# Per-token input normalisation behind two interleaved GLA blocks, a pooling map one block later, and a token-major last FFN slice, in a two-layer hybrid decoder kernel

## The chip, the cores and the metric

The kernel runs on all 8 cores of one Trainium2 chip. Each core takes one prompt of 2048 tokens and 16 samples of 8 tokens (one more tile of 128 tokens), and the cores do not exchange data. The metric is the device time of the slowest core in microseconds (us). A run is called fast when the two dies agree, and slow when the cores of one die show a lower granted TensorE clock and take longer; only fast runs are compared here. Engine names: PE is TensorE (matmul), PEld its weight loads, DVE is VectorE, ACT is ScalarE, POOL is GpSimd, SP is SyncE, which issues most transfers here.

## The reference, cut to what matters

```python
# D_MODEL = 1024, DEPTH = 2, 2048 prompt tokens per core, 16 x 8 sample tokens
def mixer_block(h, ...):
    hn = rms_norm(h, norm_mix)
    q, k, v, g_out, g_lr, xp, u, vv, gates = split(hn @ w_in)
    g_log = log_sigmoid(g_lr @ w_gk2 + b_gk) / 16
    o, s_new = gla_mix(q, k, v, g_log, s_gla)             # A: chunked scan with a state
    branch_a = (rms_norm(o) * silu(g_out)) @ w_br_a
    pool_out = pool_mix(xp, ...)                          # B: trailing windows 2/4/8/16, then a 128x128 map per group
    branch_c = (gelu(u) * (tril(w_s) @ gelu(vv) + b)) @ w_br_c   # C: chunks of 128
    merged = sum of sigmoid(gates) * branch               # with branch_b = pool_out @ w_br_b
    return h + merged @ w_out

# then  h = h + relu(rms_norm(h) @ w_ff1)**2 @ w_ff2, per layer; a final rms_norm at the end
```

## The kernel before

The 17 tiles of 128 tokens form five blocks (3, 3, 3, 4, 4 tiles; 384 or 512 tokens). Activations are kept feature-major: features on the 128 partitions, tokens along the free axis. The residual stream `hT` is fp32, and everything that the large matmuls read is bf16. Weights (1 MB each in fp32) pass through a ring of seven slots. A layer runs in stages: GLA projections for every block with the scan in the background, then mix (pooling and spatial gating), then gates and output projection, then the FFN. `tick()` moves the background work on by one step; PE itself executes strictly in the order of issue.

The start: every x tile is loaded, transposed, normed and written to DRAM before the first projection.

```python
def load_x():
    for t in range(4): xdma(t)                    # 4 x buffers of 512 KB
    rest_consts()
    for b in range(NB):
        for j in range(nt):
            for half in range(2):
                ps = psum()
                pe_transposes([...4 blocks of 128x128 of xt...], ident, ...)
                # PSUM -> hT[b], half 0 by ACT, half 1 by DVE
            xdma(t0 + j + 4)
        na = Norm(b, V_NMIX)                      # squares on ACT, summed by ones-matmuls on PE
        for m in range(KT): na.square(m)
        spill_h(b)                                # whole block to DRAM
    for b in range(NB): norm_drain(b)

def spill_h(b):
    spq.dma(h_d[b].rearrange("p (k t) -> p k t", k=KT), hT[b][:, :, :], reads=hTk[b], writes=[h_dB[b]])
```

The mix stage: the small spatial weights are loaded late, and a block's pooled tile is awaited before its map.

```python
def mix_loads(l):                                 # called at the end of the sample GLA
    spq.dma(wsp, w_spT[l] ...)                    # 128x128 per group, fp32
    spq.dma(w8, w_spT[l][:, 0:8, 0:8] ...)        # 8x8 corners for the samples
    ...
def mix_prep(l):
    tt(wsT, wsp, mask, ALU.mult, ...)             # DVE waits for wsp
    pe_group([(ps[:, 0:32], r8, w8, True, True)], ...)   # PE waits for w8
    ...
def mix_block(l, b):
    ... xp projections -> xf; pe_ = spawn(pool())  # window sums on DVE in the background
    ... u projections, vv projections with sgate(j - 1) after vgrp(j)
    drain(pe_)
    for g in range(4):
        pe_group([(ps[:, 0:T], wpm[:, g, :], pooled[:, g, 0:T], True, True)], ...)   # PE waits for pooled
        act(OBC[:, g, 0:T], ps, AF.Copy, ...)
    sgate(nt - 1)
    spq.dma(OB_d[b], OBC ...)
```

The end: the last FFN slice produces feature-major output, which is normed with ones-matmuls, scaled, transposed and stored.

```python
def ff2(l, sl, n, b):
    for m in range(KT):
        ps = proj_fm(...)                         # 8 matmuls 128 x T
        tt(hT[b][:, m, :], hT[b][:, m, :], ps, ALU.add, ...)
        if last: na.square(m)
def store_y(b):                                   # after the final norm
    for j in range(nt):
        for half in range(2):
            pe_transposes([...4 of hT[b], fp32...], ident, ...)
            act(yt[...], ps, AF.Copy, ...)
        spq.dma(rows(y_p, y_s, t0 + j), yt)
```

Of the kernel before, what the change touches and what calls it, by code (L numbers as in the profile page):

```python
# [27 lines left out]
V_NMIX, V_NFFN, V_NFIN, V_GLAN = 0, 16, 32, 40  # L28
# [70 lines left out]
def build_program():  # L99
# [28 lines left out]
    vecs = din("vecs", [128, 48])  # L128
# [53 lines left out]
    def act(out, in_, func, reads, writes, bias=None, scale=None):  # L182
        kw = {}
        if bias is not None:
            kw["bias"] = bias
        if scale is not None:
            kw["scale"] = scale
        return op(ACT, lambda: nc.scalar.activation(out=out, in_=in_, func=func, **kw), reads, writes)  # L188
# [104 lines left out]
    vec_t = sbc("vec_t", [128, 48])  # L293
# [17 lines left out]
    phist = sbc("phist", [128, 4, 15])  # L311
    fix = sbc("fix", [128, 16])
# [34 lines left out]
    xt = [sba(f"xt{i}", [128, D], F32, RA + i * 4 * KB) for i in range(4)]  # L347
# [4 lines left out]
    lvj = [part(lv, lv.t, 2 * KB * j, 2 * KB) for j in range(4)]  # L352
# [9 lines left out]
    go = sba("go", [128, KT, 512], BF16, R1 + 52 * KB)  # L362
    H4 = sba("H4", [128, KT, 512], BF16, R1 + 60 * KB)
# [20 lines left out]
    OBC = sba("OBC", [128, KT, 512], BF16, R1 + 36 * KB)  # L384
# [18 lines left out]
    ytok = [sba(f"ytok{i}", [128, D], F32, RM + 4 * KB * i) for i in range(2)]  # L403

# [9 lines left out]
    spq.dma(vec_t.t[:, :], vecs[:, :], writes=[vec_t])  # L414
# [9 lines left out]
    def rest_consts():  # L424
        spq.dma(cm.t[:, :, :], cmask[:, :, :], writes=[cm])
        spq.dma(psc.t[:, :], psc_d[:, :], writes=[psc])
        spq.dma(r8.t[:, :], r8_d[:, :], writes=[r8])
        spq.dma(mcol.t[:, :], mcol_d[:, :], writes=[mcol])
        spq.dma(invc.t[:, :, :], invc_d[:, :, :], writes=[invc])
        vcopy(ident_bf.t[:, :], ident.t[:, :], [ident], [ident_bf])  # L430
# [6 lines left out]
    def mix_consts(l):  # L437
        plq.dma(wpm.t[:, :, :], w_pm[l].rearrange("g c d -> c g d"), writes=[wpm])
        plq.dma(bsp.t[0:1, :, :], b_sp[l:l + 1], writes=[bsp])
        plq.dma(bsS.t[0:1, :, :, :], b_sp[l][:, 0:8].rearrange("(o g) t -> o g t", o=1).unsqueeze(2).broadcast_to([1, 4, NSEQ_S, LS]),  # L440
                writes=[bsS])

    def mix_loads(l):
        spq.dma(wsp.t[:, :, :], w_spT[l].rearrange("g s t -> s g t"), writes=[wsp])
        spq.dma(w8.t[:, :, :], w_spT[l][:, 0:8, 0:8].rearrange("g s t -> s g t"), writes=[w8])
# [4 lines left out]
    def mix_prep(l):  # L450
        tt(wsT.t[:, :, :], wsp.t[:, :, :], cm.t[:, 0, :].unsqueeze(1).broadcast_to([128, 4, 128]), ALU.mult, [wsp, cm], [wsT])
        ps = psum()
# [39 lines left out]
    def pump():  # L492
        while loaded[0] < len(order) and (loaded[0] < NSLOT or loaded[0] - NSLOT in retired):
# [47 lines left out]
    class Norm:  # L541
        def __init__(self, b, wcol, final=None):
            self.b, self.wcol, self.final = b, wcol, final
# [10 lines left out]
        def run(self):  # L554
# [15 lines left out]
            for kt in range(KT):  # L570
                if self.final is None:
                    dst, dB = hn_v(b)[:, kt, :], hnk[b][kt]
                else:
                    dst, dB = hT[b][:, kt, :], hTk[b][kt]
                stt(dst, hT[b][:, kt, :], vec_t.t[:, self.wcol + kt:self.wcol + kt + 1], rstd.t[:, 0:T], ALU.mult, ALU.mult,
                    [hTk[b][kt], vec_t, rstd], [dB])
                yield 1
            if self.final is not None:
                yield from self.final(b)
# [16 lines left out]

    def load_x():
        def xdma(t):
            spq.dma(xt[t % 4].t[:, :], rows(x_p, x_s, t), writes=[xt[t % 4]])
        for t in range(4):  # L600
            xdma(t)
        rest_consts()
        for b in range(NB):
            t0, nt = BLK[b]
            for j in range(nt):
                xb = xt[(t0 + j) % 4]
                for half in range(2):
                    ps = psum()
                    pe_transposes([(ps.t[:, k4 * 128:(k4 + 1) * 128], xb.t[:, (half * 4 + k4) * 128:(half * 4 + k4 + 1) * 128]) for k4 in range(4)],
                                  ident.t[:, :], [xb, ident], [ps])  # L610
                    o = hT[b][:, half * 4:half * 4 + 4, j * 128:(j + 1) * 128]
                    i = ps.t[:, :].rearrange("p (k t) -> p k t", k=4)
                    w = hTk[b][half * 4:half * 4 + 4]
                    if half == 0:
                        act(o, i, AF.Copy, [ps], w)
                    else:
                        vcopy(o, i, [ps], w)
                    tick()
                if t0 + j + 4 < NTILE:
                    xdma(t0 + j + 4)  # L620
            na = Norm(b, V_NMIX)
            norms[b] = na
            for m in range(KT):
                na.square(m)
                tick()
            spill_h(b)
        for b in range(NB):
            norm_drain(b)
# [5 lines left out]
    def gla_project(l, b):  # L634
# [5 lines left out]
        norm_drain(b)  # L640
        ps = psum()
        pe_group([(ps.t[:, 0:T], wglr.t[:, kt, :], hn_v(b)[:, kt, :], kt == 0, kt == KT - 1) for kt in range(KT)], [wglr], [ps], late=hnk[b])
        act(glr.t[0:32, 0:T], ps.t[0:32, 0:T], AF.Copy, [ps], [glr])
        tick()

        def vgrp(hf, j):
# [7 lines left out]
            act(o, ps.t[:, :], AF.Copy, [ps], [w])  # L654
            tick()

        def gate(j):
            ps = psum()
            pe_group([(ps.t[:, :], glr.t[:, j * 128:(j + 1) * 128], wgk2.t[:, :], True, True)], [glr, wgk2], [ps])
            act(lv.t[:, j, :], ps.t[:, :], AF.Exp, [ps], [lvj[j]], scale=-1.0)  # L660
            act(lv.t[:, j, :], lv.t[:, j, :], AF.Ln, [lvj[j]], [lvj[j]], bias=1.0)

        vgrp(0, 0)
        vgrp(0, 1)
        for j in range(nt):
            gate(j)
            if j >= 2:
                vgrp(0, j)
        if b == NB - 1:
            retire(l, "v0")  # L670
        for j in range(nt):
            vgrp(1, j)
        if b == NB - 1:
            retire(l, "v1")

        def cums(h):
            ps = psum()
            for j in range(nt):
                mi = 3 if (b == 0 and j == 0) else 1
                pe_group([(ps.t[:, j * 128:(j + 1) * 128], lv.t[:, j, h * 128:(h + 1) * 128], cm.t[:, mi, :], True, True)], [lvj[j], cm], [ps])  # L680
# [25 lines left out]

        cums(0)
        cums(1)
        for h in range(4):
            kgrp(h)  # L710
            qgrp(h)
            if h + 2 < 4:
                cums(h + 2)
        if b == NB - 1:
            retire(l, "k", "q")

    def gla_gate(l, b):
        T = TB[b]
        po = 128 if b == 0 else 0
        for m in range(KT):  # L720
            s, view = wget(l, "g%d" % (m // 4))
            ps = hn_fm(b, s, view, (m % 4) * 128)
            act(go.t[:, m, 0:T - po], ps.t[:, po:T], AF.Silu, [ps], [go])
# [28 lines left out]
    def gla_scan(l, b):  # L752
# [22 lines left out]
        for j in range(npr):  # L775
# [26 lines left out]
            yield from o_norm(l, OV, OB_, go.t[:, :, sl], go, H4.t[:, :, sl], H4)  # L802
# [3 lines left out]
        spq.dma(H4_d[b][:, :, po:TB[b]], H4.t[:, :, 0:TB[b] - po], reads=[H4], writes=[H4_dB[b]])  # L806
# [69 lines left out]
    def mix_block(l, b):  # L876
# [4 lines left out]
        if b == 0:  # L881
            memset(phist.t[:, :, :], 0.0, [phist])
        vcopy(xf.t[:, :, 0, 0:15], phist.t[:, :, :], [phist], [xf])
# [6 lines left out]
        vcopy(phist.t[:, :, :], xf.t[:, :, 0, Tp:Tp + 15], [xf], [phist])  # L890

# [20 lines left out]
        def pool():  # L912
            if b == 0:
                yield from pool_part(xfS, NSEQ_S, LS, 0, False)
            yield from pool_part(xf, 1, Tp, po, b == 0)

        if b == 0 or b == NB - 1:
# [9 lines left out]
        if b > 0:  # L927
            pe_ = spawn(pool())
# [5 lines left out]
        if b == 0:  # L934
# [5 lines left out]
            pe_ = spawn(pool())  # L940
# [14 lines left out]
        def sgate(j):  # L955
            smp = b == 0 and j == 0
            ps = psum()
            mms = []
            for g in range(4):
                osl = ps.t[:, g * 128:(g + 1) * 128]  # L960
                wv = wsS.t[:, g, :] if smp else wsT.t[:, g, :]
                bv = bsS.t[:, g, :, :].rearrange("o i t -> o (i t)") if smp else bsp.t[:, g, :]
                mms += [(osl, vtk.t[:, j, g * 128:(g + 1) * 128], wv, True, False, True), (osl, ones_bf.t[:, :], bv, False, True, True)]
            pe_group(mms, [vtkj[j], ones_bf] + ([wsS, bsS] if smp else [wsT, bsp]), [ps])
            tt(OBC.t[:, 4:8, j * 128:(j + 1) * 128], ps.t[:, :].rearrange("p (g t) -> p g t", g=4), uT.t[:, :, j * 128:(j + 1) * 128],
               ALU.mult, [ps, uT], [OBC])

        for j in range(nt):
            vgrp(j)
            if j > 0:  # L970
                sgate(j - 1)
        if b == NB - 1:
            retire(l, "vv")
        drain(pe_)
# [4 lines left out]
        sgate(nt - 1)  # L979
# [85 lines left out]
    def ff2(l, sl, n, b):  # L1065
# [3 lines left out]
        last = sl == 3  # L1069
        if last:  # L1070
            if b > 1:
                norm_drain(b - 2)
            na = Norm(b, V_NMIX + (l + 1) * 8) if l + 1 < DEPTH else Norm(b, V_NFIN, final=store_y)
# [10 lines left out]
        if last and l + 1 < DEPTH:  # L1084
            spill_h(b)

    def store_y(b):
        t0, nt = BLK[b]
        for j in range(nt):
            yt = ytok[(t0 + j) % 2]  # L1090
            for half in range(2):
                ps = psum()
                pe_transposes([(ps.t[:, k4 * 128:(k4 + 1) * 128], hT[b][:, half * 4 + k4, j * 128:(j + 1) * 128]) for k4 in range(4)],
# [122 lines left out]
```

## Time and profile before

Three runs gave a median of 2673.1 us: two fast ones, 2658.04 and 2673.1, and a slow one, 3045.57. In the profiled run the slowest core's span was 2655.1 us.

These are lines of the profile's page of the kernel before: busy times, the span in 40 slices (each digit is a busy share in tenths; PEclk is the granted clock in tenths), and the chain of waits by engine.

```profile
PE 2487.5 (94%) x14502; PEld 1371.0 (52%) x14502; DVE 1235.2 (47%) x2227; ACT 929.4 (35%) x1702; POOL 75.3 (3%) x94
...
PE   5798986999999999999999898699999999999997
...
PEclk7899997999999999999999999799999999999999
...
PE 86%; DMA 4%; DVE 4%; ACT 3%; issue 2%; another core or an unknown queue 0%; DVEq 0%; SPq 0%; ACTq 0%
```

PE is the bound. Its idle time and low clock lie in the first slices (start), around slices 7 and 26 (each layer's passage from GLA to mix; a slice is 66 us), and in the last slice. The view of PE's waits names the reasons (what waits, for what: us in total, times, longest):

```profile
PE ps L215 <- DVE pooled L191: 32.0, 2, 16.0
PE ps L215 <- ACT lv L188: 18.6, 24, 0.8
PE ps L215 <- DMA w<-w_spT: 16.3, 2, 9.6
...
PE ps L224 <- DMA xt_55<-xs: 8.0, 1, 8.0
PE ps L224 <- DMA xt_57<-xp: 7.0, 1, 7.0
```

The table by stretches shows the start of the slowest core (stretch, its length, then busy us and number of instructions of PE, PEld, DVE, ACT and POOL, the granted clock, the DMA share and GB/s):

```profile
0.00:100.00 100.00, 56.69 (x255) 34.19 (x255) 41.86 (x83) 43.83 (x85) 10.30 (x17) 0.80 1.02 232
100.00:133.00 33.00, 27.80 (x170) 17.27 (x171) 7.46 (x27) 8.44 (x23) 0.00 (x0) 0.90 0.73 103
```

And this is layer 1's mix stage in the same view, on core 0, from the last silu gate of the GLA projections to the first sigmoid of the gates:

```profile
1626.00:1788.00 162.00, 130.06 (x821) 73.44 (x831) 82.83 (x161) 81.38 (x141) 4.12 (x5) 0.88 0.42 91
```

So 32 of these 162 us are PE idle. Last, two groups of instructions by their form in the kernel before: first the fp32 transposes of the end, then, from the stretch 90 to 130 us, fp32 matmuls that compute a cumulative sum with a mask (count of records, busy us, mean ns of one record, which contains pipeline latency):

```profile
L224 PE MATMUL ps<-ident_t,hT_48 128*128 128x128 f32 x32 | 5.5, 348 | 3.1 <-DVE hT_48 L194 3.1
L224 PE MATMUL ps<-ident_t,hT_47 128*128 128x128 f32 x32 | 3.9, 275 | 0.9 <-DVE hT_47 L194 0.8
L224 PE MATMUL ps<-ident_t,hT_44 128*128 128x128 f32 x24 | 3.6, 273 | 0.0
...
L215 PE MATMUL ps<-cm,lv 128*128 128x128 f32 x24 | 3.8, 310 | 0.0
```

A 128x128 fp32 transpose leaves one record of roughly 0.11 us busy (3.9 us for 32).

### The profile page before, as it was taken

What the parts mean: (1) busy time and instruction counts of PE and PEld (TensorE: products, weight loads), DVE (VectorE), ACT (ScalarE), POOL (GpSimd) and SP (SyncE); (2) the same over time, 40 slices, a digit from 0 to 9 for tenths busy, and PEclk for the clock granted to TensorE, in tenths of its full rate; (3) what the DMA queues carried; (4) which work ended last, traced back from release to release, by engine and by line L of the source; (5) the groups of instructions that cost most, each with busy time, mean ns of one, the idle gap of its engine ahead of it and who ended that gap; (6) DMA issues with size and microseconds to landing.
All of it is one profiled execution on the core that took longest, in us unless ns stands there. A gap on an engine that the chain in (4) does not pass through costs nothing.

```text
span 2655.1 us, 42225 instructions; the slowest of 8 cores (2625.8 to 2655.1 us)
## 1 busy us (share of the span) xinstructions
PE 2487.5 (94%) x14502; PEld 1371.0 (52%) x14502; DVE 1235.2 (47%) x2227; ACT 929.4 (35%) x1702; POOL 75.3 (3%) x94
## 2 busy tenths in 40 slices
PE   5798986999999999999999898699999999999997
PEld 3455543554545555555555555355454555545554
DVE  3345445443435544444554545544343564444444
ACT  4366554422223321112346655542222331111144
POOL 1000000000000000000000000000000000000000
PEclk7899997999999999999999999799999999999999
DMA  9923561523518222314262347153350822221112
GB/s 243 158 88 92 117 118 48 124 88 83 117 36 195 48 33 32 48 17 65 83 131 80 100 107 128 48 109 103 74 126 32 198 49 32 33 39 27 17 49 88
DMA packets 172519, 225.72 MB, mean 85 GB/s; under 512 B 12242, under 2 KB 159866, under 8 KB 166904
## 3 DMA queue, kind: packets, MB, share of 16 engines
q0 software_dynamic: 80896, 77.97, 20.8%
q1 hardware_dynamic: 91416, 145.06, 16.9%
q8 instruction: 122, 2.00, 0.3%
q14 instruction: 85, 0.70, 0.1%
HBM read 237.46 MB, written 63.96 MB: 114 GB/s over the span
## 4 chain that ended last, share of the span: by engine, by line
PE 86%; DMA 4%; DVE 4%; ACT 3%; issue 2%; another core or an unknown queue 0%; DVEq 0%; SPq 0%; ACTq 0%
PE ps L215 85%; DMA w<-w_spT 1%; PE ps L224 1%; DMA xt_56<-xp 1%; ACT L188 1%; DMA OB_d<-OBC 1%; DMA xt_58<-xp 1%; DVE pt_101 L191 1%; DVE tmp_86 L194 0%; ACT lv L188 0%; DVE pt_102 L191 0%; ACT rsg L188 0%; DMA yp<-ytok_134 0%; DVE H_72 L191 0%
## 5 line engine op out<-in xcount | busy, mean ns | idle before, releaser
L215 PE MATMUL ps<-hn,wring 128*128 128x384 bf16 (+1 forms) x6400 | 1255.4, 350 | 12.6 <-DMA wring<-w_in 7.0
L215 PEld LDWEIGHTS ps<-hn,wring 128*128 128x128 bf16 x6400 | 625.4, 99 | 558.2 <-issue 30.0
L188 ACT ACTIVATE rl_124<-ps 128x384 f32<-128x384 f32 (+1 forms) x160 | 85.4, 534 | 498.1 <-PE ps L215 447.4
L215 PE MATMUL ps<-a_1_123,wring 128*128 128x384 bf16 (+1 forms) x1280 | 243.5, 347 | 0.0
L215 PE MATMUL ps<-a_0_122,wring 128*128 128x384 bf16 (+1 forms) x1280 | 241.2, 347 | 0.0
L215 PE MATMUL ps<-wring,hn 128*128 128x512 bf16 x848 | 206.3, 391 | 3.8 <-ACT lv L188 2.4
L215 PEld LDWEIGHTS ps<-a_1_123,wring 128*128 128x128 bf16 x1280 | 125.2, 98 | 109.9
L215 PEld LDWEIGHTS ps<-a_0_122,wring 128*128 128x128 bf16 x1280 | 125.2, 98 | 109.5
L188 ACT ACTIVATE sg_118<-ps 128x384 f32<-128x384 f32 (+1 forms) x120 | 64.1, 534 | 236.3 <-PE ps L215 156.2
L188 ACT ACTIVATE sg_119<-ps 128x384 f32<-128x384 f32 (+1 forms) x120 | 64.0, 533 | 221.2 <-PE ps L215 154.2
L188 ACT ACTIVATE rl_125<-ps 128x384 f32<-128x384 f32 (+1 forms) x160 | 85.4, 534 | 143.8 <-PE ps L215 78.5
L215 PEld LDWEIGHTS ps<-wring,hn 128*128 128x128 bf16 x848 | 82.0, 100 | 96.1 <-issue 17.1
L191 DVE TENSOR_TENSOR hT_48<-hT_48,ps 128x512 f32<-128x512 f32 x80 | 55.0, 688 | 71.4 <-PE ps L215 71.4
L191 DVE TENSOR_TENSOR hT_47<-hT_47,ps 128x512 f32<-128x512 f32 x80 | 55.0, 688 | 70.2 <-PE ps L215 70.2
L191 DVE TENSOR_TENSOR tmp_120<-sg_118,ps 128x384 f32<-128x384 f32 (+1 forms) x80 | 48.6, 607 | 81.5 <-ACT sg_118 L188 41.3
L191 DVE TENSOR_TENSOR a_0_122<-rl_124 128x384 bf16<-128x384 f32 (+1 forms) x80 | 48.9, 611 | 78.1 <-ACT rl_124 L188 78.1
L191 DVE TENSOR_TENSOR a_1_123<-rl_124 128x384 bf16<-128x384 f32 (+1 forms) x80 | 48.9, 612 | 77.0 <-ACT rl_124 L188 76.9
L191 DVE TENSOR_TENSOR tmp_121<-sg_119,ps 128x384 f32<-128x384 f32 (+1 forms) x80 | 48.5, 607 | 69.6 <-PE ps L215 35.0
L191 DVE TENSOR_TENSOR a_0_122<-rl_125 128x384 bf16<-128x384 f32 (+1 forms) x80 | 48.9, 612 | 67.6 <-ACT rl_125 L188 65.3
L191 DVE TENSOR_TENSOR a_1_123<-rl_125 128x384 bf16<-128x384 f32 (+1 forms) x80 | 48.9, 612 | 63.4 <-ACT rl_125 L188 63.4
L194 DVE SCALAR_TENSOR_TENSOR tmp_86<-ps,vec_t,rsg 128x512 f32<-128x512 f32 x68 | 51.0, 749 | 55.4 <-ACT rsg L188 51.5
L215 PE MATMUL ps<-OBs_112,wring 128*128 128x384 bf16 (+1 forms) x320 | 72.5, 349 | 3.1 <-DVE acc_114 L191 3.1
(325 smaller groups left out, 2794.9 us busy)
## 6 DMA issues: line engine op xcount, KB each, us to landing
wring<-w_ff POOLq DMA_DIRECT2D x32, 1024.0 KB, 9.1
wring<-w_in POOLq DMA_DIRECT2D x30, 1024.0 KB, 13.1
OB_d<-OBC SPq DMA_DIRECT2D x6, 768.0 KB, 4.3
H4s_110<-H_d SPq DMA_DIRECT2D x6, 768.0 KB, 8.5
OBs_112<-OB_d SPq DMA_DIRECT2D x6, 768.0 KB, 8.8
H4s_111<-H_d SPq DMA_DIRECT2D x6, 768.0 KB, 11.1
OBs_113<-OB_d SPq DMA_DIRECT2D x6, 768.0 KB, 5.0
h_d<-hT_47 SPq DMA_DIRECT2D x2, 2048.0 KB, 15.7
```

The source lines that it names most:

```text
L188: return op(ACT, lambda: nc.scalar.activation(out=out, in_=in_, func=func, **kw), reads, writes)
L191: return op(DVE, lambda: nc.vector.tensor_tensor(out=out, in0=in0, in1=in1, op=alu), reads, writes)
L194: return op(DVE, lambda: nc.vector.scalar_tensor_tensor(out=out, in0=in0, scalar=scalar, in1=in1, op0=op0, op1=op1), reads, writes)
L215: inst = nc.tensor.matmul(m[0], m[1], m[2], start=m[3], stop=m[4], **kw)
L224: inst = nc.tensor.transpose(o, i, ident_ap)
```

## The change

The change attacks all three places where PE idles, and the GLA stage on the way.

1. Start. Per-token statistics replace the ones-matmuls: ACT squares a whole token row and accumulates it, and a 128x128 matmul with a diagonal spreads the scale over partitions. The tiles are processed in the background while GLA blocks 0 and 1 are projected, interleaved. The transposed x goes to a small buffer `hx` and from there to DRAM tile by tile.
2. GLA. The silu gate has two buffers, half of the v evictions move to DVE, and a scan is not drained in a burst before the next gate.
3. Mix. The 8x8 weights are loaded at the start of the layer; the map of the pooled tile of block b is issued during block b+1.
4. End. The last FFN slice is computed token-major, with the residual added by fp32 matmuls against an identity into the same PSUM group; the final norm is then one row statistic and one scaling, and nothing is transposed afterwards.

```diff
 # start (cut)
+    def x_tile(b, j):
+        xb, hx, dg = xt[t % 3], hst_x[t % 2], diag[t % 2]
+        act(junk.t[:, :], xb.t[:, :], AF.Square, [xb], [junk, xss], acc=ss)
+        act(ss, ss, AF.Ln, ...)
+        act(ss, ss, AF.Exp, ...)
+        for half in range(2):
+            pe_transposes([...xb...], ident.t[:, :], ...)
+            act(hx.t[:, half * 4:half * 4 + 4, :], ps..., AF.Copy, [ps], [hx])
+        if t + 3 < NTILE:
+            xdma(t + 3)
+        ts(dg.t[:, :], ident.t[:, :], ss, ALU.mult, [ident, xss], [dg])
+        yield 2
+        pe_group([(ps.t[:, 0:128], ones_f.t[:, :], dg.t[:, :], True, True)], ...)
+        for kt in range(KT):
+            stt(hn_v(b)[:, kt, j * 128:(j + 1) * 128], hx.t[:, kt, :], vec_t..., ps.t[:, 0:128], ALU.mult, ALU.mult, ...)
+        spq.dma(h_d[b].rearrange("p (k t) -> p k t", k=KT)[:, :, j * 128:(j + 1) * 128], hx.t[:, :, :], reads=[hx], writes=[h_dB[b]])
+        yield 1
 # order of layer 0 (cut); p0, p1 = (low-rank gate, v0 with gates, v1, k and q) of blocks 0 and 1
+            p0[0](); p0[1]()
+            while x_done[0] < 2: tick()
+            p1[0](); p1[1](); p0[2](); p1[2](); p0[3]()
+            gla_gate(l, 0)
+            finish(x_e); pump(); gla_start(); scan(0)
+            smp_e = spawn(gla_sample(l))
+            p1[3]()
+            gla_gate(l, 1)
 # mix (cut)
+        spq.dma(w8...)                          # moved from mix_loads to mix_consts
 def mix_block(l, b):
+        if b > 0: drain(pool_e[0])
         ... xp projections ...
+        if b > 0: mix_finish(l, b - 1)          # pooled map of the block before
 # end (cut)
+    def ff2_last(l, n, b):
+        for j in range(nt):
+            for half in range(2):
+                mms = [(ps.t[:, :], a.t[:, kt, sl], view[:, kt, :], kt == 0, False, True) for kt in range(KT)]
+                mms += [(ps.t[:, c * 128:(c + 1) * 128], hT[b][:, half * 4 + c, sl], ident.t[:, :], False, True, True) for c in range(4)]
+                act(yjunk.t[:, :], ps.t[:, :], AF.Square, [ps], [yjunk, ss], acc=ss.t[:, half:half + 1])
+            ... two tiny ACT steps: Ln, Exp ...
+            for half in range(2):
+                stt(yt.t[:, hs], pss[half].t[:, :], ss.t[:, 0:1], wfin.t[:, hs], ALU.mult, ALU.mult, ...)
+            spq.dma(rows(y_p, y_s, t), yt.t[:, :], reads=[yt])
```

## The prediction

> **What bounds the kernel now.** TensorE: the page gives PE 2487.5 us busy of 2655.1 (94%), and the chain of waits runs 86% over PE. In the table by stretches PE is 99 to 100% busy at clock 1.00 from 530 to 1260 and from 1800 to 2600 us. The 168 us of PE idle, and the low clock, lie elsewhere:
>
> 1. Start: 0 to 133 us holds only 84 us of PE busy (clock 0.74, then 0.90). All activations are loaded, normed and spilled before the first projection at 78 us. PE's waits: x tiles 28 us, weights 7, ACT about 9. DMA is full until 120 us.
> 2. GLA to mix, per layer. PE waits 9.6 us (layer 0) and 6.7 (layer 1) for the 8x8 spatial weights, queued behind 1 MB weight loads; 16.0 us for the pooled tile in both layers (DVE runs window sums without pause); 5.9 us for ACT vtk, which stands behind DVE. The clock falls to 0.50 to 0.75.
> 3. Tail: the last FFN matmul ends at 2631 us; 24 us of scaling, transposes, evictions and stores follow.
>
> Within GLA small waits (ACT lv 9.3 us per layer) and the scan emitted in a burst cost about 18 us per layer.
>
> **What the change does.**
> - Start: per-row statistics (one 1024-wide ACT square per tile) replace 40 matmuls of 0.32 to 0.38 us; x tiles run behind the projections of blocks 0 and 1. But 6 MB of weights, 8.9 MB of x and 8.9 MB of spill must still cross a DMA that was full to 120 us, and the in-order PE ties projections to arriving x tiles (three buffers, not four). I expect the start to end near 115 us with block 1's gates and v done: 25 to 30 us saved, not 60.
> - GLA: double-buffered silu gate, no scan burst, half of the v evictions on DVE (0.6 us each): 5 to 8 us per layer.
> - Mix: the small weights come early, but wsp still stands behind weight loads and blocks DVE (14.6 us in layer 0), so half of that wait goes; mapping a block later hides most of the 16 us. DVE stays nearly as loaded as PE; I keep 5 to 10 us of waits. Gain with recovered clock: 25 to 30 us per layer.
> - Tail: 136 fp32 transposes become 136 fp32 residual matmuls (both 0.11 us); 40 norm matmuls (7.3 us) go. After the last matmul remain a square, tiny steps, two 0.75 us scalings and a 2.7 us store: 7 us instead of 24. Gain 24 us.
>
> Sum: 27 + 13 + 54 + 24 = 118 us off 2655, all critical, since PE idles there.
>
> The Trainium skill, "TensorE: Matmul & The Clock Gate" (Part 1), says that the clock halves after an idle window and returns after some 3.4 us of busy time; the trace agrees (clock 0.50 from 410 to 420 us, after 16 us idle). So a removed wait returns a little more than itself.
>
> **Prediction: 2540 us**, 2500 to 2585 in 8 of 10 cases. Chances: faster by over 2% 0.94, within 2% 0.05, slower 0.01.
>
> **Right if** PE's waits for pooled and the 8x8 weights are gone; projections start before 30 us and PE is over 75% busy in 0 to 133 us; the span ends within 10 us of the last matmul; PE busy falls by 40 to 60 us.
>
> **Wrong if** v0 arrives late and stalls PE together with the x tiles (start of 130 us or more, total near 2570); the DVE wait for wsp or pooling returns as a wait of xf in the next block; Silu and Ln/Exp alternate and table loads (1.28 us each) hold ACT back; or, the other way, the start ends near 90 us (total near 2510).

## The result, and the profile after

The kernel after is correct. Its median was 2639.07 us (four fast runs, 2636.26 to 2640.0) against 2670.49 us for the kernel before in the same rounds. The ratio is 0.9896, with a 95% interval of 0.9859 to 0.9932. Ratios here are the mean time of one kernel's fast runs over that of the other's of the same rounds, so they are not quite the ratio of the quoted medians. A second comparison with more rounds gave 0.9934 (0.9918 to 0.995). The change saves about 18 us of the 118 us that were predicted.

The page of the kernel after, the same lines:

```profile
PE 2484.8 (94%) x14544; PEld 1377.7 (52%) x14544; DVE 1241.0 (47%) x2329; ACT 915.5 (35%) x1731; POOL 75.5 (3%) x94
...
PE   3879978999999999999999898899999999999998
...
PEclk7989999999999999999999999999999999999999
...
PE 83%; DMA 5%; ACT 5%; DVE 4%; issue 2%; SPq 0%; DVEq 0%; ACTq 0%
```

The dip at the passage to mix has become shallower in both layers, and the clock there is back. But the first slice fell from 5 to 3, and PE's busy time fell by only 3 us, where 40 to 60 was expected. PE's waits:

```profile
PE ps L218 <- ACT lv L191: 16.1, 21, 0.8
PE ps L218 <- ACT xfS L191: 15.0, 2, 7.7
PE ps L227 <- ACT hx_58 L191: 12.2, 1, 12.2
PE ps L218 <- DVE tmp_92 L197: 10.1, 7, 2.5
```

The waits for `pooled` and for the 8x8 weights are gone, as predicted. New are `xfS` (once per layer, first mix block) and `hx`, the small buffer of the start. The start by stretches, and layer 1's mix stage on core 0:

```profile
0.00:100.00 100.00, 50.14 (x209) 29.40 (x210) 29.23 (x100) 35.09 (x75) 10.48 (x17) 0.80 1.00 187
100.00:133.00 33.00, 31.06 (x213) 21.98 (x210) 19.48 (x79) 28.01 (x62) 0.00 (x0) 1.00 0.67 184
```

```profile
1617.00:1760.00 143.00, 126.35 (x810) 70.78 (x819) 80.91 (x157) 76.26 (x133) 4.13 (x5) 0.95 0.43 95
```

PE does less work in the first 100 us than before (50 us instead of 57). The mix stage is 19 us shorter on this core, and 17 of its 143 us are still PE idle.

To see where the time went, I read the same events of every core's trace in both profiled runs: the last silu gate of block 1, the last silu gate of the GLA projections, the first sigmoid of the gates, and the last ACT instruction. For each event I took the median of its time over the eight cores; the table gives the differences between these medians.

| Stretch | before, us | after, us | difference | predicted |
|---|---|---|---|---|
| start to block 1's silu gate | 176.3 | 183.9 | +7.6 | −27 |
| block 1's gate to end of GLA, layer 0 | 187.3 | 191.2 | +3.9 | about −6 |
| GLA end to gates (mix), layer 0 | 155.7 | 140.1 | −15.6 | −27 |
| gates of layer 0 to end of GLA, layer 1 | 1107.4 | 1106.2 | −1.2 | about −6 |
| GLA end to gates (mix), layer 1 | 153.6 | 142.4 | −11.2 | −27 |
| gates of layer 1 to the end | 862.1 | 860.9 | −1.2 | −24 |

The start lost time, the mix stages gave half of what was predicted, and the end gave almost nothing. The last point is odd, because the visible tail did shrink. This is the timeline of the kernel after at its end (start us, length us, instruction):

```profile
2625.03 1.89 PE L218 MATMUL ps<-wring,a_1_130 128*128 128x512 bf16 x8
...
2626.76 1.05 PE L218 MATMUL ps<-ident_t,hT_48 128*128 128x128 f32 x8
...
2629.68 1.60 DVE L197 SCALAR_TENSOR_TENSOR ytok_141<-ps,yss_145,wfin 128x512 f32<-128x512 f32 x2 [0.76 <-ACT yss_145 L191]
2631.36 0.33 SPq L165 DMA_DIRECT2D yp<-ytok_141  x1
```

The last matmul ends at 2627.8 us and the span at 2635.2: 7.4 us of tail instead of 24, close to the 7 predicted. The timeline also shows what paid for it. Each half tile needs four residual matmuls, and the trace has eight records for them. The groups by form in the kernel after confirm it:

```profile
L218 PE MATMUL ps<-ident_t,hT_48 128*128 128x128 f32 x64 | 8.4, 275 | 0.0
...
L218 PE MATMUL ps<-ident_t,hT_44 128*128 128x128 f32 x48 | 6.3, 275 | 0.0
```

Before, the same tensors had 32 and 24 records for as many transposes.

### The profile page after: what moved, and what is told of

The parts are those of the page before. It is cut to its first block, busy times and chain, and to the rows that moved or that the text cites. A ratio compares the mean times of both kernels' runs of the same rounds, so it can differ in the third digit from the quotient of the medians.

```text
span 2635.2 us, 42566 instructions; the slowest of 8 cores (2619.9 to 2635.2 us)
## 1 busy us (share of the span) xinstructions
PE 2484.8 (94%) x14544; PEld 1377.7 (52%) x14544; DVE 1241.0 (47%) x2329; ACT 915.5 (35%) x1731; POOL 75.5 (3%) x94
## 4 chain that ended last, share of the span: by engine, by line
PE 83%; DMA 5%; ACT 5%; DVE 4%; issue 2%; SPq 0%; DVEq 0%; ACTq 0%
PE ps L218 83%; DMA h_d<-hx_59 2%; ACT L191 1%; DMA wsp<-w_spT 1%; DMA h_d<-hx_58 1%; DVE tmp_92 L197 1%; DMA OB_d<-OBC_110 1%; ACT rsg L191 1%; ACT lv L191 0%; DVE pt_107 L194 0%; PE ps L227 0%; ACT OBC_110 L191 0%; DVE pt_108 L194 0%; DVE go_77 L194 0%; ACT junk L191 0%
## 5 line engine op out<-in xcount | busy, mean ns | idle before, releaser
L218 PE MATMUL ps<-a_0_129,wring 128*128 128x384 bf16 (+1 forms) x1152 | 215.3, 347 | 0.0
L218 PE MATMUL ps<-a_1_130,wring 128*128 128x384 bf16 (+1 forms) x1088 | 205.9, 348 | 0.0
L218 PEld LDWEIGHTS ps<-a_0_129,wring 128*128 128x128 bf16 x1152 | 112.7, 98 | 98.3
L218 PEld LDWEIGHTS ps<-a_1_130,wring 128*128 128x128 bf16 x1088 | 106.4, 98 | 94.4
L194 DVE TENSOR_TENSOR hT_48<-hT_48,ps 128x512 f32<-128x512 f32 x72 | 49.5, 688 | 63.7 <-PE ps L218 63.7
L194 DVE TENSOR_TENSOR hT_47<-hT_47,ps 128x512 f32<-128x512 f32 x72 | 49.5, 688 | 62.2 <-PE ps L218 62.2
L218 PE MATMUL ps<-OBs_119,wring 128*128 128x384 bf16 (+1 forms) x320 | 73.0, 351 | 5.3 <-DVE acc_121 L194 5.3
L191 ACT ACT_TABLE_LOAD x49 | 62.9, 1283 | 40.5 <-PE ps L218 31.8
```

The costliest lines, as they stand in the source:

```text
L191: return op(ACT, lambda: nc.scalar.activation(out=out, in_=in_, func=func, **kw), reads, writes)
L194: return op(DVE, lambda: nc.vector.tensor_tensor(out=out, in0=in0, in1=in1, op=alu), reads, writes)
L218: inst = nc.tensor.matmul(m[0], m[1], m[2], start=m[3], stop=m[4], **kw)
```

## Experiments

Theories after reading the two traces:

- T1, end: an fp32 residual matmul costs PE two records of 0.11 us and not one. Rival: the token-major slice is slow because ACT and DVE hold its PSUM banks.
- T2, start: the spills of `hx` hold up ACT and then PE. They are written in pieces of 512 B, because a tile is 128 tokens of 4 B per feature row within its block, and they compete with the weight loads. Rivals: too few buffers; alternation of activation tables; the new order itself.
- T3, mix: what remains comes from DVE waiting for `wsp`, after which the first mix block starts late. Rival: DVE simply has too much work in the first mix blocks.

All experiments are edits of the kernel after. Three groups ran on three chips, each with its own runs of the kernel before; the kernel after ran only in the first. "Against after" below is therefore (ratio of the experiment − 0.9934) × 2656 us, which assumes that the kernel after stands in the same relation to the kernel before on each chip. Both intervals enter this column: it is uncertain by about 6 us where the experiment's interval is narrow, and by 9 to 13 us for e4 to e7. The intervals of e4, e6 and e7 overlap that of the kernel after, and e8's just does.

The second group (e4 to e7) needs one more caution. In several of its runs that are counted as fast, some cores of both dies were granted a lower clock (mean 0.964 to 0.973). If only runs are taken in which every core's mean clock is at least 0.975, e4 has one (2628.94 us), e6 one (2627.43), e7 three (2623.71 to 2630.41) and e5 three (2652.54 to 2664.22). The kernel after has seven in its two comparisons, 2636.26 to 2641.3 us. By these few runs e4, e6 and e7 are each about 10 us faster than the kernel after, and e5 is about 19 us slower; for e4, e6 and e7 the column below therefore understates the gain. This is an estimate from few runs, and choosing by the clock favours quick runs; the kernel before's fast runs are alike in both groups (mostly 2653 to 2660 us).

| Run | ratio to before, 95% | us against after | result |
|---|---|---|---|
| a0_after | 0.9934 (0.9918 to 0.995) | 0 | correct |
| e1_no_residual | 0.983 (0.9814 to 0.9846) | −28 | wrong |
| e2_residual_bf16 | 0.9846 (0.9832 to 0.986) | −23 | correct |
| e3_start_undone | 0.9871 (0.9853 to 0.989) | −17 | correct |
| e4_four_hx | 0.9952 (0.991 to 0.9995) | +5 | correct |
| e5_spill_rows | 1.0007 (0.9978 to 1.0037) | +19 | correct |
| e6_wsp_early | 0.9908 (0.986 to 0.9956) | −7 | correct |
| e7_gate_after_x | 0.9908 (0.9873 to 0.9943) | −7 | correct |
| e8_no_sample_sums | 0.9906 (0.989 to 0.9921) | −7 | wrong |
| e9_rows_rearranged | 0.9856 (0.9841 to 0.9872) | −21 | correct |
| e10_all | 0.9693 (0.9679 to 0.9706) | −64 | correct |
| e11_oldstart_bf16 | 0.9791 (0.9777 to 0.9804) | −38 | correct |

### a0_after: the change again, with more rounds

No edit.

> The changed kernel again, as the reference of this chip for the runs beside it. Ratio to before 0.985 to 0.994, as in the first comparison (0.9896).

Measured: 0.9934. The gain is real but small, about 18 us.

### e1_no_residual: no residual matmuls (wrong result)

```diff
-                mms = [(ps.t[:, :], a.t[:, kt, sl], view[:, kt, :], kt == 0, False, True) for kt in range(KT)]
-                mms += [(ps.t[:, c * 128:(c + 1) * 128], hT[b][:, half * 4 + c, sl], ident.t[:, :], False, True, True) for c in range(4)]
+                mms = [(ps.t[:, :], a.t[:, kt, sl], view[:, kt, :], kt == 0, kt == KT - 1, True) for kt in range(KT)]
```

> The changed kernel without the residual matmuls of the last slice (wrong y on purpose, all else as it is). My theory for the tail: one fp32 residual matmul leaves two records of 0.11 us on PE, not one as a transpose does, so the 136 of them cost 30 us on a PE that never idles there. Expected: 27 to 31 us faster than the changed kernel, span about 2606 us. Rival: the tail gained little because PE waits on psum banks held until the scaling (two per token tile); then removing the matmuls gives 15 us or less, since the waits stay.

Measured: 28 us faster than the kernel after. 272 records at 0.11 us are an estimate of 30 us; 136 records would be 15. The ACT and DVE steps on each PSUM bank stayed, so the rival is refuted.

### e2_residual_bf16: the residual in bf16, correct

```diff
+    hTb = [nc.alloc_sbuf_tensor_at(f"hTb{b}", [128, KT, 2 * TB[b]], BF16, offset=hoff[b]) for b in range(NB)]
 # FFN slice before the last one, last layer: write the residual as bf16
-            tt(hT[b][:, m, :], hT[b][:, m, :], ps.t[:, 0:T], ALU.add, ...)
+            tt(hTb[b][:, m, 0:T] if l == DEPTH - 1 and sl == 2 else hT[b][:, m, :], hT[b][:, m, :], ps.t[:, 0:T], ALU.add, ...)
-                mms += [(..., hT[b][:, half * 4 + c, sl], ident.t[:, :], False, True, True) for c in range(4)]
+                mms += [(..., hTb[b][:, half * 4 + c, sl], ident_bf.t[:, :], False, True, True) for c in range(4)]
```

> The changed kernel with the hidden state written as bf16 by slice 2's add (same place, same instruction count) and the residual added through bf16 matmuls. If the fp32 passes are the cost: each residual matmul falls from 0.22 to 0.055 us, 136 of them save 22 us; total 20 to 24 us faster than the changed kernel, and still a correct result. If psum banks or ACT set the pace of the last slice: under 8 us.

Measured: 23 us faster than the kernel after. The group by form in this kernel:

```profile
L218 PE MATMUL ps<-ident_bf,hTb 128*128 128x128 bf16 x136 | 13.1, 219 | 0.0
```

Now 136 matmuls leave 136 records. Their busy time is 13.1 us; in the kernel after the five fp32 groups sum to 35.7 us (two of 8.4, three of 6.3). The difference of 22.6 us is the measured gain. The Trainium skill, "FP8 and Floating Point Precision" (section "TensorE Precision Notes"), says that true fp32 takes four passes through the array. This agrees in the total: 0.22 us for the two records of one fp32 matmul against 0.055 us for a bf16 matmul of this width (an estimate: a quarter of the spacing at width 512, where eight matmuls take 1.89 us in the timeline above with some 0.17 us of latency at the end). T1 holds.

### e3_start_undone: the old start, with the rest of the change

```diff
-    xt = [... for i in range(3)]
+    xt = [... for i in range(4)]
-    def x_tile(b, j): ...
+    def load_x(): ...            # as in the kernel before: blocks loaded, normed and spilled first
-        if l == 0: ...           # interleaving of blocks 0 and 1 removed
```

> The changed kernel with the start of before (x all loaded, normed by column sums and spilled ahead of the first projection, four x buffers, all seven weight slots at once); the GLA, mix and tail parts of the change stay. Theory: the new start gains nothing, because its x tiles stand behind spills that stand behind weights; undoing it costs between -5 and +5 us. The prediction's claim, that the new start is worth 25 to 30 us, would make this run 25 to 30 us slower than the changed kernel.

Measured: 17 us faster than the kernel after, where −5 to +5 was expected. So the new start, as built, costs 17 us and does not gain 27. Block 1's silu gate ends at 174.3 us here (183.9 after), and the stretch from there to the end of GLA takes 183.0 us (191.2 after, 187.3 before). The second half of the loss is therefore paid after the start: the new order postpones scans and sample states into later blocks. Without that, the GLA change saves 4 us in layer 0.

### e4_four_hx: four buffers in place of two

```diff
+    hst_x += [sba(f"hx{2 + i}", [128, KT, 128], F32, SC + i * 4 * KB) for i in range(2)]
-        xb, hx, dg = xt[t % 3], hst_x[t % 2], diag[t % 2]
+        xb, hx, dg = xt[t % 3], hst_x[t % 4], diag[t % 2]
```

> The changed kernel with four transposed-tile buffers in the start instead of two, so that a tile need not wait for the spill of the tile two before it. If that wait (53 us of ACT waiting for the spill of hx in the trace) is what slows the start: 10 us or more faster than the changed kernel (ratio to before 0.989 or less). Rival, DMA volume: the spills and weights only move the wait on to the x loads (three buffers), under 4 us.

Measured: unclear (0.9952; its interval overlaps that of the kernel after, and some cores were disturbed). The profiled run gives a better answer on its undisturbed die (cores 4 to 7): block 1's silu gate ends at 178.7 us, against 185.1 on the same cores of a0_after. So the two extra buffers are worth some 6 us at this milestone, and about 10 us by the one undisturbed run: between the two expectations. The rest of the wait moved. In the kernel after, ACT's waits in the first 155 us are led by these two:

```profile
ACT hx_59 L191 <- DMA h_d<-hx_59: 27.4, 3, 13.7
ACT hx_58 L191 <- DMA h_d<-hx_58: 25.5, 2, 13.8
```

With four buffers the same view, same stretch, shows the input loads in their place; below them stands the longest wait of SP, which issues both the loads and the spills, in order:

```profile
ACT junk L191 <- DMA xt<-xp: 23.5, 4, 11.0
PE ps L227 <- DMA xt<-xp: 22.1, 5, 11.2
...
SPq L49 <- DMA h_d<-hx: 65.7, 10, 15.2
```

SP stands 65.7 us waiting for earlier spills to land before it may issue the next one, and the x loads behind it wait too. So the number of `hx` buffers is a small part of the cause. The number of x buffers (three in place of four) was never tested.

### e5_spill_rows: the spill written as rows of 4 KB

```diff
+    hx_d = [dtmp(f"hx_d{t}", [128, KT * 128], F32) for t in range(NTILE)]
-        spq.dma(h_d[b].rearrange("p (k t) -> p k t", k=KT)[:, :, j * 128:(j + 1) * 128], hx.t[:, :, :], reads=[hx], writes=[h_dB[b]])
+        spq.dma(hx_d[t].rearrange("p (k t) -> p k t", k=KT), hx.t[:, :, :], reads=[hx], writes=[hx_dB[t]])
 # h_load of layer 0 reads tile by tile from hx_d (34 transfers of 256 KB)
```

> The changed kernel with each x tile spilled to its own place in DRAM in rows of 4 KB instead of 512 B pieces (and read back tile by tile in the layer's output projection). If the small pieces make the spill slow under load: spill landings fall from 14 to 26 us in the first 90 us, 5 to 12 us faster than the changed kernel. If the weights in front are the cause and not the size: within 3 us.

Measured: 19 us slower in all, where a gain was expected, in two parts that the trace separates. Block 1's silu gate ends at 160.9 us in place of 185.1 (a0_after): the start is 24 us shorter. But the stretch from the first gate to the FFN takes 397.9 us in place of 359.3: 39 us longer. First, queues and issues of the kernel after between 15 and 75 us (packets, MB and share of the engines' time; then KB and median us from issue to landing):

```profile
q1 hardware_dynamic: 4871, 4.34, 28.2%
...
h_d<-hx_59 SPq DMA_DIRECT2D x2, 512.0 KB, 21.9
...
h_d<-hx_58 SPq DMA_DIRECT2D x2, 512.0 KB, 15.8
```

The same of this experiment, and below it ACT's wait for the spill in the first 155 us, then a wait of the stretch 520 to 900 us:

```profile
q1 hardware_dynamic: 2099, 7.51, 35.9%
...
hx_d<-hx SPq DMA_DIRECT2D x8, 512.0 KB, 10.7
...
ACT hx L191 <- DMA hx_d<-hx: 15.3, 6, 4.4
...
DVE hT L194 <- DMA hT<-hx_d: 54.7, 8, 15.5
```

While the weights load, the kernel after moves 4.3 MB on this queue, in packets of 0.9 KB on average (4.34 MB over 4871), and the experiment moves 7.5 MB, in packets of 3.6 KB, in the same time. ACT's wait falls from 53 us to 15.

But the edit removed two things at once. In the kernel after, all spills of a block write under one name, `h_dB[b]`, and the helper that orders transfers holds each write back until the last write under that name has landed, although the pieces do not overlap. The experiment gives each tile a name of its own, `hx_dB[t]`. SP's waits in the first 155 us of the kernel after show this (core 7):

```profile
SPq L49 <- DMA h_d<-hx_59: 27.4, 3, 15.4
...
SPq L49 <- DMA h_d<-hx_58: 15.1, 3, 12.6
```

These 42.5 us, during which the x loads stood behind the spill too, are not there in the experiment. So the 24 us belong to the short pieces and to this one-at-a-time issue together. The pieces alone do land late (15.8 to 21.9 us against 10.7, with fewer of them under way), and the median time of a packet on SP's queue (kernel after, 15 to 75 us) was 40 ns for 512 B and 172 ns for 4 KB, so a long one moves nearly twice as many bytes in its time. No run has short pieces without the waiting, or rows with it: the split stays open.

On the other side, the tile-by-tile read-back makes DVE wait 55 us before the residual additions of the output projection. Here too it is the order of issue: the 34 loads write under shared names, and SP waited 24 times, 103 us in all, for the load before, while each landed in 3.0 us (median). T2 holds for the start as far as the spill path is the cause; the first attempt to use it paid more elsewhere.

### e6_wsp_early: the spatial weights loaded at the start of the layer

```diff
+        plq.dma(wsT.t[:, :, :], w_spT[l].rearrange("g s t -> s g t"), writes=[wsT])     # in mix_consts
-        spq.dma(wsp.t[:, :, :], w_spT[l].rearrange("g s t -> s g t"), writes=[wsp])     # in mix_loads
-        tt(wsT.t[:, :, :], wsp.t[:, :, :], mask, ALU.mult, [wsp, cm], [wsT])
+        tt(wsT.t[:, :, :], wsT.t[:, :, :], mask, ALU.mult, [wsT, cm], [wsT])
```

> The changed kernel with the large spatial weights loaded (cast by the DMA) into their final place at the start of the layer, so that the mask on DVE waits for no DMA at the start of the mix stage. Theory: PE's wait for ACT xfS (7.7 us in layer 0, less in layer 1), which stands behind that DVE wait, goes: 8 to 14 us faster than the changed kernel over both layers. Rival: the pooling history, loaded at the same moment behind the same weights, takes over as the wait: under 4 us.

Measured: 7 us faster than the kernel after, though the intervals overlap; the one undisturbed run gives about 11. In the kernel after, the passage to mix of layer 1 (1615 to 1735 us) has this chain of waits:

```profile
ACT xf L191 <- DVE xf L203: 17.0, 4, 9.3
...
DVE wsT_p L194 <- DMA wsp<-w_spT: 11.1, 1, 11.1
...
PE ps L218 <- ACT xfS L191: 7.2, 1, 7.2
```

DVE stands 11 us at the mask for a transfer, ACT waits for the history that DVE should copy, and PE waits for ACT. In the experiment DVE's wait for the weights is gone in both layers and PE's wait for `xfS` is 0.3 us in layer 0 and no longer listed in layer 1. Layer 1's mix stage takes 135.2 us in place of 142.6, as it should. Layer 0's takes 142.2 in place of 141.2 by the medians over all cores, but here the profiled run was disturbed: four cores (2 to 5) were granted a clock of 0.81 from 408 us on, for 160 us, and they take 148.4 to 148.7 us. The other four, granted 0.99, take 135.5 to 135.7. So on undisturbed cores the edit gains some 6 us in layer 0 as well, about 12 us in all, which is within what was expected.

### e7_gate_after_x: tile processing finished before the silu gate

```diff
             p0[3]()
-            gla_gate(l, 0)
+            p1[3]()
             finish(x_e)
+            gla_gate(l, 0)
             ...
             smp_e = spawn(gla_sample(l))
-            p1[3]()
```

> The changed kernel with the order in the start changed: k and q of block 1 run before the silu gate of block 0, and the gate only after the last x tile, so that Silu and Ln/Exp do not alternate. Theory: the 6 table loads between 121 and 140 us (1.28 us each) and the PE idle of about 10 us there go, 5 to 10 us faster than the changed kernel. Rival: the end of the start is set by the DMA before 90 us and nothing is saved: within 3 us.

Measured: 7 us faster than the kernel after, intervals overlapping; the three undisturbed runs give about 11. In the kernel after, six activation table loads fall between 100 and 150 us (median over the cores), because silu gates alternate with the Ln and Exp of x tiles; here one does. Block 1's silu gate ends 20 us earlier (165.5 us against 185.1). A load takes 1283 ns, so five avoided loads explain about 6.4 us of busy time; the rest is the other order, and partly work put off: PE was busy for 112 us by that milestone, against 119 to 121 in the kernel after. But the stretch from the last silu gate to the first u projection grows from 19.0 to 33.9 us: the sample states, started later, now end the GLA stage. Table loads are a small part of the start's loss. The Trainium skill, "ScalarE: Activation LUTs" (section "What ACT_TABLE_LOAD costs"), gives about 1283 ns for the load, as this trace does, and another 1380 ns of drain, which no run here isolates.

### e8_no_sample_sums: less DVE work in the first mix block (wrong result)

```diff
-                    tt(nxt[...], cur[...], cur[...], ALU.add, [curB], [nB])
-                    cur, curB = nxt, nB
+                    if nseq == 1:
+                        tt(nxt[...], cur[...], cur[...], ALU.add, [curB], [nB])
+                        cur, curB = nxt, nB
```

> The changed kernel without the ten window sums per layer of the sample rows (pooling result wrong on purpose): 4.6 us of DVE work less per layer, in the first two blocks of the mix stage. If DVE is what holds PE there: 3 to 5 us less per layer, 6 to 10 us in all. If DVE has room and PE waits for something else: under 3 us.

Measured: 7 us faster than the kernel after, by intervals that just touch. The removed window sums are 4.6 us of DVE time per layer, and the mix stages shrink by 4.1 and 3.7 us. Nearly all of the DVE time removed in the first mix blocks comes back in time, so the rival of T3 is also right: at that place DVE sets the pace.

### e9_rows_rearranged: rows of 4 KB, put in order in DRAM later

This is e5 with the layout restored by DRAM-to-DRAM copies during the first gate blocks of layer 0, so that the read-back is again one large transfer.

```diff
+        if l == 0:                                   # in gate_block
+            for t in range(2 * n, min(2 * n + 2, NTILE)):
+                spq.dma(h_d[bt]...[:, :, j * 128:(j + 1) * 128], hx_d[t]..., reads=[hx_dB[t]], writes=[h_dB[bt]])
```

> As e5 (x tiles spilled in 4 KB rows), but put into the layout of before by DRAM to DRAM copies during the gate stage, where DMA has room, so that the output projection reads it back as before. The start of e5 was 24 us shorter than that of the changed kernel (end of block 1's silu gate at 161 against 185 us), and its gate and output stages 38 us longer. If the read-back was what cost: 18 to 26 us faster than the changed kernel, ratio to before 0.984 to 0.987. If the copies slow the gate stage's weight loads: no gain.

Measured: 21 us faster than the kernel after. Block 1's silu gate ends at 161.1 us, as in e5, and the stretch from the first gate to the FFN takes 358.9 us, as in the kernel after. The start by stretches:

```profile
0.00:100.00 100.00, 68.92 (x372) 44.52 (x373) 45.47 (x166) 53.12 (x115) 10.37 (x17) 0.90 1.03 220
```

PE does 69 us of work in the first 100 us, in place of 50, at a clock of 0.90 in place of 0.80. The copies still move 512 B pieces, and still wait for one another at SP (51 us), but at a place where nothing else waits for them. Like e5, this run removes the short pieces and the one-at-a-time issue together.

### e10_all: the corrections together

e9, e2 and e6, with this order of the start:

```diff
             p0[3]()
-            gla_gate(l, 0)
+            p1[3]()
             finish(x_e)
             pump()
             gla_start()
-            scan(0)
             smp_e = spawn(gla_sample(l))
-            p1[3]()
+            gla_gate(l, 0)
+            scan(0)
             gla_gate(l, 1)
             scan(1)
```

> All that helped together: spill in rows with the copies of e9, bf16 residual, spatial weights early, block 1's k and q ahead of block 0's gate with the sample states started before that gate. Expected from the parts: 22 (residual) + 22 (spill) + 7 (weights) + 0 to 8 (order) = 51 to 59 us faster than the changed kernel, ratio to before 0.971 to 0.975. If the parts overlap (the copies collide, or the sample states become the end of GLA as in e7): 30 to 45 us.

Measured: median 2575.87 us with two slow runs among six; the fast ones lie from 2570.68 to 2578.71. The ratio to the kernel before is 0.9693, so this correct version is 3.1% faster than the kernel before and beats both kernels. The 64 us exceed the expectation and the sum of e9, e2 and e6 as tabled (51); the table understates e6, and the new order of the start was tested only in the form of e7, so the excess is not split further. Block 1's silu gate ends at 150.2 us, and PE's busy time is down to 2450.5 us, from 2484.8.

### e11_oldstart_bf16: e3 and e2 together

The edits of e3 and e2.

> The changed kernel with the start of before and the bf16 residual: the two repairs that need no new layout. Both were measured apart (16 and 23 us faster than the changed kernel) and lie at opposite ends, so 36 to 40 us faster, ratio to before 0.978 to 0.980.

Measured: 38 us faster than the kernel after; e3 and e2 alone gave 17 and 23, so the two causes add up. It is 26 us slower than e10_all, which differs by the repaired spill, the new order of the start and the earlier spatial weights. With 7 to 12 us for the weights (e6), 14 to 19 are left for the new start in e10's order. The repaired spill alone is worth less over the old start: e9 is only 4 us faster than e3, with overlapping intervals. The rest would come from e10's order, which no run isolates.

## Why the prediction was right or wrong

The predicted total was 2540 us, and the measured one about 2639. The reading of the kernel before was right: PE bound, with idle time in the start, the passage to mix, and the tail. Each term of the sum failed in its own way.

**Start, predicted 25 to 30 us saved, measured 8 us lost at block 1's silu gate.** The step that failed reads "I expect the start to end near 115 us with block 1's gates and v done: 25 to 30 us saved". The milestone itself was met: block 1's last v eviction ends at 103 us (median over the cores). Its worth was wrong. By 103 us PE had done 53 us of work in the profiled core. In the kernel before, the same eviction ends only at 147 us, but PE had done 57 us of work by 100 us and 99 by then: the interleaving pulled block 1's v forward and pushed block 0's k, q and silu gate, the scan and most x tiles back. The prediction took a milestone of the new order for the end of a stage of the old one. It did name the DMA as full, but it costed the spill by bytes. The spills, in pieces of 512 B and one at a time, held ACT for 53 us and PE for one stretch of 12 us without work. The timeline of the kernel after shows such a moment:

```profile
16.22 0.54 SPq L165 DMA_DIRECT2D h_d<-hx_59  x1
...
33.66 0.52 SPq L165 DMA_DIRECT2D h_d<-hx_58  x1
33.67 1.29 ACT L191 ACTIVATE hx_59<-ps 128x512 f32<-128x512 f32 x2 [13.67 <-DMA h_d<-hx_59]
...
37.99 10.75 SPq L165 DMA_DIRECT2D xt_56<-xp  x1
...
50.71 1.29 ACT L191 ACTIVATE hx_58<-ps 128x512 f32<-128x512 f32 x2 [13.76 <-DMA h_d<-hx_58]
51.45 1.09 PE L227 MATMUL ps<-ident_t,xt_57 128*128 128x128 f32 x4 [12.22 <-ACT hx_58 L191]
```

The spill of `hx_59` is issued at 16.2 us and lands at about 33.7, which releases both ACT and the next spill. That one had its tile ready at 18.1 us, and waited. The next x load is then stuck for 10.75 us at its issue, ACT gets the buffer only at 50.7 us, and PE follows. That this spill path, short pieces and one-at-a-time issue together, costs 24 us at the same milestone is shown by e5 and e9; the share of each is not shown, and that short pieces suffer by taking turns with the weight packets is only an inference. e3 puts the new start's total cost at 17 us: 8 at the gate, the rest later. The Trainium skill, "DMA: Bandwidth & Descriptors" (section "Queues, rings and completion order"), says that each engine goes round the queues packet by packet; nothing here isolates that. Two of the prediction's "wrong if" cases occurred: a start of 130 us or more (the last x tile leaves PE at 137 us and ACT at 142, medians), and table loads, which e7 shows to be the smaller part.

**GLA, predicted 5 to 8 us per layer, measured 4 us in layer 0 and about 3 in layer 1.** The direction was right, about half the size. Layer 1's figure lies within a row of the table: from the FFN's start in layer 0 to the end of GLA in layer 1 the kernel after takes 746.2 us and the kernel before 748.9, while gates and output projection of layer 0 take 1.5 us more. Layer 0's gain shows only with the old start (e3); in the kernel after, postponed scans and sample states take it back. The small waits for ACT `lv` hardly changed (18.6 to 16.1 us). I tested none of the three parts of this change alone, so their shares stay open.

**Mix, predicted 25 to 30 us per layer, measured 16 and 11.** The mechanism was right: both large waits are gone and the clock is back (0.88 to 0.95 in layer 1's mix stage). This fits the Trainium skill, "TensorE: Matmul & The Clock Gate" (Part 1), on which the prediction drew: after an idle window the clock is halved. The mis-sized term is "I keep 5 to 10 us of waits": 17 us of PE idle remained on the core shown. The prediction even named the reason among its "wrong if" cases, that the DVE wait for `wsp` returns as a wait for xf; it does, in both layers (7.7 and 7.2 us at PE), though in the first block and not in the next one. e6 removes it and gains 6 to 7 us per layer on undisturbed cores; e8 shows that DVE's work paces what is left.

**End, predicted 24 us saved, measured 1.** The step that failed is "136 fp32 transposes become 136 fp32 residual matmuls (both 0.11 us)". The residual matmul takes two records, 0.22 us. There was also a double count: 64 of the 136 transposes, 9.4 us of busy time, lay inside the old tail of 24 us, whose disappearance was counted already. The account from the traces closes: the tail is 17 us shorter and 7.3 us of ones-matmuls go; against that, fp32 identity work ahead of the last matmul rises from 10.8 us (three groups of 3.6) to 35.7. The sum is about zero, as measured. The kernel before held the clue: its cumulative sums show 24 records for 12 matmuls.

In the sum: predicted 118, measured about 18. Of the 100 us missing, e2 and the start's repair e9 return 44, and e10_all returns 64.

## What to carry to other kernels

Price a matmul with the trace's records of a matmul of the same type, and count records per instruction issued: a transpose with an identity is not priced like a matmul with the same identity. When a stage is reordered, compare the work that PE has done by a given time rather than when one milestone is passed, and check for every small transfer moved into a loaded stretch how long its contiguous pieces are, and for which earlier transfers its issue has to wait: bookkeeping by block puts pieces in a row that could fly together. Before a run is explained, look at the granted clock of each core. If a layout must change, let it be changed where nobody waits for it.

## What the Trainium skill lacked or had wrong

- "FP8 and Floating Point Precision" (section "TensorE Precision Notes") gives four passes for true fp32 but does not say that a trace shows one fp32 matmul as two records (272 for 136 here, 0.11 us each), nor that an fp32 transpose with an identity takes one record of 0.11 us, half of that.
- "TensorE: Matmul & The Clock Gate" (section "Terms") calls the transpose mode four times faster for fp32, without saying than what. Here an fp32 128x128 transpose took half the time of an fp32 matmul of the same size (0.11 against 0.22 us); no run shows whether these transposes use that mode.
- "DMA: Bandwidth & Descriptors" (section "Specifications") gives 512 B as the smallest transfer for line rate. In these runs pieces of exactly 512 B were slower beside weight loads: a packet of 512 B took 40 ns at the median and one of 4 KB 172 ns, so per byte the short one took nearly twice as long, and spills landed in 15.8 to 21.9 us in place of 10.7.
- The same page has nothing on the issue of a local transfer being held up: one took 10.75 us on SP's queue just after two spills of 512 B pieces, where 0.33 us is usual in this trace. That the small pieces caused it is an inference.
